# Output projection and feed-forward with activations stationary and 512 weight columns moving, norms by token row

## The chip, the cores and the metric

The kernel runs on one core of one Trainium2 chip. The metric is device time in microseconds for one execution; the time before is the median of three runs. Durations inside the execution come from the hardware profiler's record of one execution. The engines are named as the profile names them: PE (matrix products), PEld (its weight loads), DVE (vector), ACT (activation), POOL, and SP, whose queue issues the DMAs here.

## The reference

One layer of a decoder trunk over 256 tokens and 2048 channels, float32, with weights that are read once from HBM. What is computed, shortened:

```
mod = silu(c) @ w_mod + b_mod                       # 6 x 2048 values, from one vector c
sh1, sc1, g1, sh2, sc2, g2 = split(mod, 6)
u = x * (1 + sc1) + sh1
y = token_mixer(u)                                  # u @ w_in, mLSTM and HGRN2 heads, then ... @ w_out (2048 x 2048)
x = layer_norm(ALPHA * x + (1 + g1) * y, ln1_g, ln1_b)
u = x * (1 + sc2) + sh2
y = (silu(u @ w_gate) * (u @ w_up)) @ w_down        # 2048 x 5632 twice, 5632 x 2048
out = layer_norm(ALPHA * x + (1 + g2) * y, ln2_g, ln2_b)
```

Each product in float32 is made of three: an operand is split into a high part (rounded to fp32r) and a low part (the rest), and high x high, high x low and low x high are summed in PSUM.

## The kernel before

**Stages.** The input projection and the two head groups come first (the tile names `uh`, `ul`, `wh`, `wl`, `q`, `kk`, `pr`); then the output projection from `yh`, `yl` (high and low part of the mixer's output), the first norm, the modulation that makes `u2`, the feed-forward in two halves of 22 blocks of 128 hidden channels (gate and up first, then down), the second norm and the output.

**Weights.** Every weight tile is 128 x 1024 (512 KB). `wtile` (L206) lets SP fetch it into `wr`, ACT makes the high part `wh` from it (recorded at L128, the helper `act`), and DVE the low part `wl` by a subtraction (L213). There are 4 buffers for `wr`, 4 for `wh` and 3 for `wl`.

**Matrix products.** In the output projection and the feed-forward the weights are stationary, 128 x 128 at a time, and 256 tokens of activations move: `gB` (L243, matmuls L249 to L251), and the same three matmuls written out at L859 to L861 (the first 8 blocks of the feed-forward) and L872 to L874 (the others). Values are therefore held by channel: a channel is a partition, a token a column. `gA` (L253, matmuls L260 to L262) is the other form: 128 tokens of activations are stationary, 512 weight columns move; before the change only the parts `i` and `v` of the input projection use it.

**Norms.** As channels lie on partitions, a norm over channels needs sums across partitions: class `Norm` makes them by matmuls with a matrix of ones in plain float32 (L733, L774, L776) and applies them with L817 and L819 (first norm) or L903 and L904 (second).

**The modulation products.** The 96 values per partition of `mod` come one column at a time: `mod(j)` (L171) fetches 128 x 2048 of `w_mod` (1 MB) into one of 2 buffers `m`, and one DVE instruction (L174) multiplies it with `silu(c)` and sums. Columns 0 to 31 belong to u, 32 to 47 and 64 to 79 to the first gate and the second scale (`modq`, drawn by `mods_some` at rates RATE per step), 48 to 63 to the second shift (`make_u2`), 80 to 95 to the second gate, which only the feed-forward's down part needs.

**Order.** No order is written out by hand. A scheduler sorts the instructions of each engine by priorities, dependencies and its own estimate of times when the program is built; each engine then runs its list in that order, and SP issues its DMAs in one list as well. So where the 96 modulation products stand on DVE and in SP's list is the scheduler's result.

Of the kernel before, what the change touches and what calls it, by code (L numbers as in the profile page):

```python
# [9 lines left out]
P = 128  # L10
# [44 lines left out]
RATE = (0.3, 0.2, 0.3)  # L55
CFG = dict(big=10, med=10, wr=4, mr=2, wh=4, wl=3, s5=2, t=3, cm=2)
# [23 lines left out]
def build(nc, tc, d):  # L80
    from contextlib import ExitStack

    with ExitStack() as ctx:
# [70 lines left out]
        for n in (128, 256, 768, 2048):  # L154
            ones[n] = cst.tile([P, P], F32, name=f"ones{n}")
            nc.gpsimd.memset(ones[n], 1.0 / n)
# [527 lines left out]
        wo = [0]  # L684

        def next_wo():
            i = wo[0]
            wo[0] += 1
            return (wraw if i // 4 % 2 == 0 and i % 4 in NATIVE[i // 8] else wtile)(d["wo"][i])

        xa = [A(name="xa") for _ in range(2)]
        for i in range(4):
            o = xa[i // 2][:, 1024 * (i % 2) : 1024 * (i % 2) + 1024]
            nc.sync.dma_start(o, d["x"][i])
            act(o, o, AF.Copy, scale=ALPHA)
        z = [A(name="z") for _ in range(2)]

        def b8(ap, n=8):
            return ap.rearrange("p (o t) -> p o t", o=1).broadcast_to([P, n, T])

        class Norm:
            def __init__(self, z, base, gcol, dve):
                self.z, self.base, self.gcol, self.dve = z, base, gcol, dve
                self.todo = []
                self.n = 0

            def put(self, b, bank):
                for j in range(2):
                    o = kt(self.z, b + j)
                    stt(o, bank[:, j * T : j * T + T], self.gcol(b + j), kt(self.base, b + j), ALU.mult, ALU.add)  # L710
                if b == 4:
                    self.todo.append(self.shift)
                if b == 6:
                    self.shifted()
                    for k in range(0, 8, 2):
                        self.todo.append(lambda k=k: self.sums(k))
                if b >= 8:
                    self.todo.append(lambda: self.sums(b))

            def tick(self):  # L720
                for f in self.todo:
                    f()
                self.todo = []

            def total(self, o, n, tiles, first=True, last=True):
                if self.dve and len(tiles) > 2:
                    a = S(T, "t", bufs=CFG["t"])
                    tt(a, tiles[0], tiles[1], ALU.add)
                    for t in tiles[2:]:
                        tt(a, a, t, ALU.add)  # L730
                    tiles = [a]
                for i, t in enumerate(tiles):
                    mm(o, ones[n], t, start=first and i == 0, stop=last and i == len(tiles) - 1, skip_group_check=True)  # L733

            def shift(self):
                s = ps()
                self.total(s[:, :T], 768, [kt(self.z, k) for k in range(6)])
                self.sh = M(T, name="nsh")
                act(self.sh, s[:, :T], AF.Copy)

            def shifted(self):
                for t in (self.z[0], self.base[1]):
                    for i in range(0, 2048, 512):
                        v = v3(t[:, i : i + 512], 2)
                        tt(v, v, b8(self.sh, 2), ALU.subtract)

            def sums(self, b):
                if b == 0:
                    self.mu, self.ss = ps(), ps()
                    self.ma = self.sa = None  # L750
                    if self.dve:
                        t = M(512, name="nacc")
                        self.ma, self.sa = t[:, :T], t[:, T:]
                q = S(512, "s5", bufs=CFG["s5"])
                act(q, self.z[b // 8][:, (b % 8) * T : (b % 8) * T + 512], AF.Square)
                zs = [kt(self.z, b), kt(self.z, b + 1)]
                qs = [q[:, :T], q[:, T:]]
                if self.dve and b < 14:
                    if b == 6:
                        tt(self.ma, zs[0], zs[1], ALU.add)  # L760
                    elif b > 6:
                        for x in zs:
                            tt(self.ma, self.ma, x, ALU.add)
                    if b == 0:
                        tt(self.sa, qs[0], qs[1], ALU.add)
                    else:
                        for x in qs:
                            tt(self.sa, self.sa, x, ALU.add)
                    return
# [42 lines left out]
        def make_u2(k):  # L812
# [7 lines left out]
            if k == 0:  # L820
                table["first"] = i
# [150 lines left out]
```

## Time and profile before

| | |
|---|---|
| three runs | 1304.82, 1308.33, 1306.6 us; median 1306.6 |
| profiled execution: span from first to last instruction | 1303.7 us (no other time of this execution is listed) |
| PE / DVE / ACT busy | 1258.4 / 911.6 / 615.6 us |
| mean TensorE clock granted | 0.991 of 2.4 GHz |
| HBM read | 320.59 MB, 248 GB/s over the span |

The page divides the span into 40 slices and gives the busy share of each engine in tenths. A record of a matmul lasts longer than the distance to the next one, because matmuls are pipelined; how fast PE works is read from the starts of neighbouring records, not from the duration of one. A plain float32 matmul leaves two records. In a chain of records of one kind the timeline merges neighbours and writes xN.

### The profile page before, as it was taken

The numbers are of one execution on the slowest core, as the hardware profiler recorded it, in microseconds if no ns is written. First come the engines' busy times: TensorE is split into PE (matmuls) and PEld (weight loads), VectorE is DVE, ScalarE is ACT, GpSimd is POOL, SyncE is SP. The second block draws the span as 40 slices with busy tenths as digits, with TensorE's granted clock in tenths as the row PEclk, the third lists the DMA queues.
The fourth block names the chain that finished last, engine by engine and source line by source line (L and its number), as shares of the span: only waits on it lengthen the run. The fifth ranks groups of instructions, "written<-read, shape, count | busy, mean of one in ns | idle before, by whom it ended". The sixth has DMA issues, their size and how long they took to land.

```text
span 1303.7 us, 24455 instructions
## 1 busy us (share of the span) xinstructions
PE 1258.4 (97%) x10184; PEld 1224.8 (94%) x10184; DVE 911.6 (70%) x1079; ACT 615.6 (47%) x810; POOL 4.1 (0%) x15
## 2 busy tenths in 40 slices
PE   4899999999999999999999999999999999999995
PEld 4889999898989999999999999999999999999995
DVE  6779977999898897998876544444544544545755
ACT  4564446546655633654444443333444444443444
POOL 0000000000000000000000000000000000000000
PEclk9899999999999999999999999999999999999998
DMA  9988997756988889699896556656555656556561
GB/s 368 373 339 335 350 387 260 253 184 203 347 292 324 330 323 327 239 322 339 307 345 223 184 173 184 186 179 190 189 179 181 190 179 182 189 171 183 178 190 73
DMA packets 76863, 324.28 MB, mean 249 GB/s; under 512 B 8528, under 2 KB 8912, under 8 KB 64336
## 3 DMA queue, kind: packets, MB, share of 16 engines
q1 hardware_dynamic: 76752, 322.73, 71.6%
q8 instruction: 79, 1.29, 0.4%
q14 instruction: 32, 0.26, 0.1%
HBM read 320.59 MB, written 2.10 MB: 248 GB/s over the span
## 4 chain that ended last, share of the span: by engine, by line
PE 93%; DVE 4%; ACT 1%; issue 1%; DMA 1%; ACTq 0%; DVEq 0%
PE ps L249 14%; PE ps L251 14%; PE ps L250 14%; PE ps L874 11%; PE ps L873 11%; PE ps L872 11%; PE ps L860 2%; PE ps L861 2%; PE ps L859 2%; PE ps L261 2%; PE ps L260 2%; PE ps L262 2%; DVE m L174 2%; PE ps L445 1%; DVE wl L213 1%
## 5 line engine op out<-in xcount | busy, mean ns | idle before, releaser
L213 DVE TENSOR_TENSOR wl<-wr,wh 128x1024 fp32r<-128x1024 f32 (+1 forms) x416 | 498.5, 1203 | 326.9 <-PE ps L874 154.3
L128 ACT ACTIVATE wh<-wr 128x1024 fp32r<-128x1024 f32 (+1 forms) x416 | 432.6, 1042 | 541.1 <-PE ps L250 223.5
L872 PE MATMUL ps<-wh,wh 128*128 128x256 f32 x1152 | 326.0, 283 | 0.0
L873 PE MATMUL ps<-wl,wh 128*128 128x256 f32 x1152 | 326.0, 283 | 0.0
L874 PE MATMUL ps<-wh,wl 128*128 128x256 f32 x1152 | 326.0, 283 | 0.0
L174 DVE CUSTOM_DVE_ANT_0 m<-m,cb,init 128x2048 f32<-128x2048 f32 x96 | 225.0, 2347 | 15.1 <-DMA m<-in_wmod 14.7
L872 PEld LDWEIGHTS ps<-wh,wh 128*128 128x128 f32 x1152 | 221.2, 192 | 0.0
L873 PEld LDWEIGHTS ps<-wl,wh 128*128 128x128 f32 x1152 | 221.2, 192 | 0.0
L874 PEld LDWEIGHTS ps<-wh,wl 128*128 128x128 f32 x1152 | 221.2, 192 | 0.0
L249 PE MATMUL ps<-uh,wh 128*128 128x256 f32 x640 | 185.1, 294 | 22.0 <-ACT wh L128 16.8
L249 PE MATMUL ps<-h,wh 128*128 128x256 f32 x704 | 199.4, 283 | 0.0
L251 PE MATMUL ps<-h,wl 128*128 128x256 f32 x704 | 199.2, 283 | 0.0
L250 PE MATMUL ps<-h,wh 128*128 128x256 f32 x704 | 199.2, 283 | 0.0
L250 PE MATMUL ps<-ul,wh 128*128 128x256 f32 x640 | 182.3, 287 | 0.0
L251 PE MATMUL ps<-uh,wl 128*128 128x256 f32 x640 | 181.0, 288 | 1.1 <-DVE wl L213 1.0
L249 PEld LDWEIGHTS ps<-uh,wh 128*128 128x128 f32 x640 | 124.3, 196 | 24.7 <-ACT wh L128 17.2
L250 PEld LDWEIGHTS ps<-h,wh 128*128 128x128 f32 x704 | 135.2, 192 | 0.0
L249 PEld LDWEIGHTS ps<-h,wh 128*128 128x128 f32 x704 | 135.2, 192 | 0.0
L251 PEld LDWEIGHTS ps<-h,wl 128*128 128x128 f32 x704 | 135.2, 192 | 0.0
L250 PEld LDWEIGHTS ps<-ul,wh 128*128 128x128 f32 x640 | 125.2, 196 | 1.1 <-issue 1.0
L251 PEld LDWEIGHTS ps<-uh,wl 128*128 128x128 f32 x640 | 123.8, 195 | 2.0 <-DVE wl L213 1.8
L859 PE MATMUL ps<-wh,wh 128*128 128x256 f32 x256 | 71.6, 284 | 2.9 <-ACT wh L128 2.9
(203 smaller groups left out, 1484.5 us busy)
## 6 DMA issues: line engine op xcount, KB each, us to landing
m<-in_wmod SPq DMA_DIRECT2D x96, 1024.0 KB, 6.9
wr<-in_wg SPq DMA_DIRECT2D x144, 512.0 KB, 3.6
wr<-in_win SPq DMA_DIRECT2D x112, 512.0 KB, 5.3
wr<-in_wd SPq DMA_DIRECT2D x80, 512.0 KB, 3.5
wr<-in_wo SPq DMA_DIRECT2D x32, 512.0 KB, 5.0
wr<-in_wf SPq DMA_DIRECT2D x32, 512.0 KB, 5.2
wr<-in_wd SPq DMA_DIRECT2D x16, 256.0 KB, 2.6
xT<-in_x SPq DMA_DIRECT2D x4, 512.0 KB, 7.8
```

The source lines that it names most:

```text
L128: i = nc.scalar.activation(out, in_, f, **kw).ins
L174: table["mod"] = nc.vector.tensor_tensor_reduce(t, t, cb, 1.0, init[:, j : j + 1], ALU.mult, ALU.add, modc[:, j : j + 1]).ins
L213: tt(l[:, :m], r[:, :m], h[:, :m].bitcast(F32), ALU.subtract)
L249: mm(o, h[:, wsl], kt(uh, k0 + k), start=st, stop=False, skip_group_check=True)
L250: mm(o, h[:, wsl], kt(ul, k0 + k), start=False, stop=False, skip_group_check=True)
L251: mm(o, l[:, wsl], kt(uh, k0 + k), start=False, stop=en, skip_group_check=True)
L260: mm(o, a, h[:, w], start=first and k == 0, stop=False, skip_group_check=True)
L261: mm(o, a, l[:, w], start=False, stop=False, skip_group_check=True)
L859: mm(o, h[:, wsl], kt(u2h, k), start=k == 0 and w == 0, stop=False, skip_group_check=True)
L872: mm(o, h[:, wsl], kt(u2h, kk), start=kk == 0 and w == 0, stop=False, skip_group_check=True)
L873: mm(o, h[:, wsl], kt(u2l, kk), start=False, stop=False, skip_group_check=True)
L874: mm(o, l[:, wsl], kt(u2h, kk), start=False, stop=kk == KT - 1, skip_group_check=True)
```

## The change

- In the output projection and the feed-forward the operands change places. `three` (L709) takes 128 tokens of activations as the stationary operand and moves 512 columns of the weights, with two matmuls for the high part of the weights (L712, L713) and one for the low part (L716). Each of the two token halves t has banks of its own.
- Values are now held by token: a token is a partition. The residual is made by rows (`resid`, L723 with L725 or L727), the sums of the norm by DVE's statistics instructions (L730, L734), and the norm is applied by rows (L792, L935, L936). `z` holds x by rows. The ones-matrix matmuls of both norms go.
- A gate that was a column is now needed along the row: `bcast` (L689, L694) lays it out over 128 partitions by 16 plain float32 matmuls.
- The next product needs channels on partitions again, so PE transposes: 8 x 4 tiles for u2 (`make_u2`, L799) and 4 x 2 tiles for each of the 11 groups of 512 hidden channels (`flip`, L835).
- Skew: the last column group of the output projection does token half 0 before half 1; the first two k-steps of the feed-forward run for half 0 before half 1's u2 is made; the last two k-steps of the down part too.
- The feed-forward goes group by group: groups 0 and 1 together in 8 banks, then one group at a time; the down part follows groups 0 to 5 and then 6 to 10. The layer norm's weights come along the row by a broadcasting DMA (`spill`).
- RATE goes from (0.3, 0.2, 0.3) to (0.4, 0.3, 0.4); `wh` and `wl` get 5 buffers each, `s5` 4.

```diff
-RATE = (0.3, 0.2, 0.3)
-CFG = dict(big=10, med=10, wr=4, mr=2, wh=4, wl=3, s5=2, t=3, cm=2)
+RATE = (0.4, 0.3, 0.4)
+CFG = dict(big=10, med=10, wr=4, mr=2, wh=5, wl=5, s5=4, t=3, cm=2)
...
-        n1 = Norm(z, xa, lambda k: col(2, k), False)
-        for half in range(2):
-            banks = [ps() for _ in range(4)]
...
+        def three(banks, h, l, a, b, first, last):
+            for i, o in enumerate(banks):
+                w = slice(512 * i, 512 * i + 512)
+                mm(o, a, h[:, w], start=first, stop=False, skip_group_check=True)
+                mm(o, b, h[:, w], start=False, stop=False, skip_group_check=True)
+            for i, o in enumerate(banks):
+                w = slice(512 * i, 512 * i + 512)
+                mm(o, a, l[:, w], start=False, stop=last, skip_group_check=True)
...
+        def norm(t):
+            mv = S(4, f"mv{t}", bufs=1)
+            nc.vector.bn_aggr(mv[:, 0:2], st[t])
+            act(mv[:, 2:3], mv[:, 1:2], AF.Ln, bias=eps)
+            table["var"] = act(mv[:, 3:4], mv[:, 2:3], AF.Exp, scale=-0.5)
+            return mv[:, 0:1], mv[:, 3:4]
...
         run(modq)
...
+        for k in range(EARLY):
             run(mod(48 + k))
-            if k >= EARLY:
-                tc.add_manual_dep(table["mod"], table["first"].name, order, reason="norm")
...
+        def make_u2(t, c):
+            bank = ps()
+            for j in range(4):
+                nc.tensor.transpose(bank[:, P * j : P * j + P], z[t][:, 512 * c + P * j : 512 * c + P * j + P], ident)
+            for j in range(4):
+                k = 4 * c + j
+                if t == 0 and k >= EARLY:
+                    run(mod(48 + k))
+                    tc.add_manual_dep(table["mod"], table["first"].name, order, reason="norm")
+                o = bank[:, P * j : P * j + P]
+                h = u2(u2h, k, t)
+                act(h, o, AF.Identity, scale=Ac[:, k : k + 1], bias=col(3, k))
+                u = S(P, "t", bufs=CFG["t"])
+                ts(u, o, Ac[:, k : k + 1], col(3, k), ALU.mult, ALU.add)
+                tt(u2(u2l, k, t), u, h.bitcast(F32), ALU.subtract)
...
+        norm1(0)
+        use = False
+        for c in range(4):
+            make_u2(0, c)
+        norm1(1)
...
+        bk, held, block = ffn_in((0, 1))
+        for k in range(2):
+            for g in range(2):
+                held[k, g] = w1(d["wf"][g * KT + k])
+            block(k, 0)
+        for c in range(4):
+            make_u2(1, c)
+        for k in range(2):
+            block(k, 1)
+        for k in range(2, KT):
+            for g in range(2):
+                held[k, g] = w1(d["wf"][g * KT + k])
+            for t in range(2):
+                block(k, t)
...
+        up_to(range(2, 6))
+        G2 = bcast(5)
+        down(0, 24, G2, False)
+        up_to(range(6, NG))
+        use_set(AF.Exp)
+        Lg, Lb = spill("l2g"), spill("l2b")
+        down(24, 44, G2, True)
```

How the scheduler lays this out is told by the order of the two programs. First DVE in the kernel before, at the seam between the output projection and the feed-forward: `wl` is the low part of a weight tile (the first row is the feed-forward's third), L710 the last residual, L782 to L819 the norm, L826 the low part of u2, L174 a modulation product.

```order
L213 TENSOR_TENSOR wl_5449<-wr_5446,wh_5448 128x1024
L710 SCALAR_TENSOR_TENSOR z_4228<-ps_4756,modc,xa_4218 128x256 x2
L782 TENSOR_TENSOR nrs_5335<-ps_4821,nrs_5335 128x256
L817 TENSOR_TENSOR z_4227<-z_4227,nmu_5334 128x256 x4
L819 TENSOR_TENSOR z_4227<-z_4227,nrs_5335 128x256 x4
...
L213 TENSOR_TENSOR wl_5479<-wr_5476,wh_5478 128x1024
L819 TENSOR_TENSOR z_4227<-z_4227,nrs_5335 128x256
L174 ISA m_5920,modc<-m_5920,cb,init 128x2048
L174 ISA modc 128x1
L213 TENSOR_TENSOR wl_5518<-wr_5515,wh_5517 128x1024
```

The third, fourth and fifth feed-forward tiles' low parts stand here with one modulation product among them. Now DVE in the changed kernel at the same seam: `wl_5248` is the low part of the feed-forward's fifth weight tile, `wl_5254` of its sixth; L723 with ps_4498 makes the last residual of token half 1, L792 applies the norm, L809 and L810 make u2's low part (`u2l_4928` holds four k of it), L884 scales z for the second residual.

```order
L706 TENSOR_TENSOR wl_5248<-wr_5245,wh_5247 128x1024
L727 SCALAR_TENSOR_TENSOR z_4228<-z_4228,s_4907 128x512
L723 TENSOR_TENSOR s_4911<-ps_4498,bc_4234 128x512
...
L792 TENSOR_SCALAR z_4228<-z_4228,mv_4956 128x512 x4
L174 ISA m_5011,modc<-m_5011,cb,init 128x2048
L174 ISA modc 128x1
L809 TENSOR_SCALAR t_4970<-ps_4964,sc,modc 128x128
L174 ISA m_5018,modc<-m_5018,cb,init 128x2048
...
L810 TENSOR_TENSOR u2l_4928<-t_5143,u2h_4924 128x128
L174 ISA m_5871,modc<-m_5871,cb,init 128x2048
...
L706 TENSOR_TENSOR wl_5254<-wr_5251,wh_5253 128x1024
```

Between the fifth tile's subtraction and the sixth's stand 100 rows, and no weight tile is among them: 14 modulation products, 50 instructions of 128 columns (L809, L810), 21 of 512 columns (a row with x4 counted four times) and four of the statistics. One more modulation product stands right after the last residual of half 0 (`s_4907`), ahead of the low parts of tiles 2 to 5.

Last PE in the changed kernel at this place: L716 with ps_4498 ends the output projection (half 1), L799 are the transposes of z_4228 (half 0) and z_4229 (half 1), u2h_4924 and u2l_4928 belong to k 0 to 3; wl_5092 is the low part of the feed-forward's first tile, wl_5248 of its fifth, wh_5253 the high part of its sixth, ps_5086 a bank of half 1.

```order
L716 MATMUL ps_4498<-wl_4856,yh_4210 128x512
L799 MATMUL ps_4964<-kc,z_4228 128x128 x4
...
L713 MATMUL ps_5081<-wh_5091,u2l_4928 128x512
...
L716 MATMUL ps_5082<-wl_5248,u2h_4924 128x512
L799 MATMUL ps_5158<-kc,z_4229 128x128 x4
...
L716 MATMUL ps_5086<-wl_5092,u2h_4924 128x512
...
L712 MATMUL ps_5083<-wh_5253,u2h_4924 128x512
```

From the end of the output projection to the first matmul with the sixth tile stand the 32 transposes and 45 feed-forward matmuls: tiles 1 to 5 with half 0 (30) and 15 with half 1. Before, all 8 banks followed the norm with the first k at once, and no transpose was between.

## Rows read from the trace of the kernel before

**Rows 1.** The page: busy time of each engine, and the span in 40 slices (tenths of busy time; PEclk is the granted clock).

```profile
PE 1258.4 (97%) x10184; PEld 1224.8 (94%) x10184; DVE 911.6 (70%) x1079; ACT 615.6 (47%) x810; POOL 4.1 (0%) x15
...
PE   4899999999999999999999999999999999999995
...
DVE  6779977999898897998876544444544544545755
...
PEclk9899999999999999999999999999999999999998
DMA  9988997756988889699896556656555656556561
```

**Rows 2.** Busy time of each engine in four stretches: start and end, length, then PE, PEld, DVE, ACT, POOL with counts, the granted clock, the share of the DMA engines, GB/s. They are about the output projection, the feed-forward, what follows it, and the time right after the feed-forward's start.

```profile
417.00:524.00 107.00, 104.36 (x812) 101.31 (x810) 89.73 (x110) 52.46 (x60) 0.00 (x0) 1.00 0.88 324
524.29:1286.70 762.41, 762.41 (x6339) 762.32 (x6340) 451.54 (x525) 329.18 (x397) 0.00 (x0) 1.00 0.64 208
1286.70:1303.70 17.00, 2.92 (x14) 1.91 (x12) 11.02 (x19) 10.35 (x21) 0.00 (x0) 0.71 0.32 124
...
525.34:529.56 4.22, 4.22 (x25) 4.22 (x24) 3.14 (x8) 3.33 (x5) 0.00 (x0) 0.60 0.00 0
```

**Rows 3.** PE in order of time (start, duration, engine, line, tiles, sizes): the first and the last of 44 single records in the feed-forward, 256 columns each.

```profile
999.84 0.28 PE L873 MATMUL ps<-wl,wh 128*128 128x256 f32 x1
...
1005.00 0.28 PE L874 MATMUL ps<-wh,wl 128*128 128x256 f32 x1
```

**Rows 4.** The same view in the input projection: the first and the last of 23 single records of the form with 512 weight columns moving.

```profile
328.83 0.39 PE L261 MATMUL ps<-wl,uh 128*128 128x512 f32 x1
...
333.82 0.39 PE L262 MATMUL ps<-wh,ul 128*128 128x512 f32 x1
```

**Rows 5.** The same view: plain float32 matmuls, which leave two records each, with the next instruction behind them; 128 columns (L492) and 256 columns (L733, the ones matrix).

```profile
309.79 1.05 PE L492 MATMUL ps<-q,kk 128*128 128x128 f32 x8
310.60 0.48 PE L260 MATMUL ps<-wh,uh 128*128 128x512 f32 x1
...
460.65 2.75 PE L733 MATMUL ps<-z,ones 128*128 128x256 f32 x12
463.05 0.47 PE L249 MATMUL ps<-yh,wh 128*128 128x256 f32 x1
```

**Rows 6.** The same view at the start of the output projection: the last mLSTM head's matmuls, the first output projection matmul, and the head's last sums.

```profile
413.64 0.36 PE L249 MATMUL ps<-yh,wh 128*128 128x256 f32 x1
...
416.47 0.61 PE L587 MATMUL ps<-s,ones 128*128 128x256 f32 x2
```

**Rows 7.** The same view at the seam: the last output projection matmul, the last norm sums, the first feed-forward matmuls with the idle time before them.

```profile
517.10 0.28 PE L251 MATMUL ps<-yh,wl 128*128 128x256 f32 x1
...
520.27 1.13 PE L776 MATMUL ps<-s,ones 128*128 128x256 f32 x4
524.29 1.22 PE L859 MATMUL ps<-wh,wh 128*128 128x256 f32 x8 [2.89 <-ACT wh L128]
```

**Rows 8.** DVE in order of time behind the seam: steps of 256 columns, then a modulation product with its read-out and the weight subtraction behind it.

```profile
521.85 1.42 DVE L817 TENSOR_TENSOR z<-z,nmu 128x256 f32<-128x256 f32 x4
523.19 1.42 DVE L819 TENSOR_TENSOR z<-z,nrs 128x256 f32<-128x256 f32 x4
...
530.19 2.35 DVE L174 CUSTOM_DVE_ANT_0 m<-m,cb,init 128x2048 f32<-128x2048 f32 x1
532.46 0.08 DVE L174 DVE_READ_ACCUMULATOR2_ANT modc<- 128x1 f32 x1
532.46 1.22 DVE L213 TENSOR_TENSOR wl<-wr,wh 128x1024 fp32r<-128x1024 f32 x1
533.60 1.09 DVE L826 TENSOR_TENSOR wl<-t,wh 128x256 fp32r<-128x256 f32 x3
```

**Rows 9.** DVE's modulation products early in the kernel, in order of time: the first and the last of eight that stand close together.

```profile
9.32 2.35 DVE L174 CUSTOM_DVE_ANT_0 m<-m,cb,init 128x2048 f32<-128x2048 f32 x1
...
37.51 2.35 DVE L174 CUSTOM_DVE_ANT_0 m<-m,cb,init 128x2048 f32<-128x2048 f32 x1 [0.17 <-DMA m<-in_wmod]
```

**Rows 10.** The page's DMA issues: size of one, median us from issue to landing.

```profile
m<-in_wmod SPq DMA_DIRECT2D x96, 1024.0 KB, 6.9
```

**Rows 11.** The end of the kernel in order of time, PE, DVE and ACT: the last feed-forward matmul, steps of 512 columns of the last norm, the last DVE and ACT records.

```profile
1286.58 0.28 PE L251 MATMUL ps<-h,wl 128*128 128x256 f32 x1
...
1295.67 1.28 DVE L903 TENSOR_TENSOR z<-z,nmu 128x512 f32<-128x512 f32 x2
1296.88 1.28 DVE L904 TENSOR_TENSOR z<-z,nrs 128x512 f32<-128x512 f32 x2
...
1298.80 0.69 DVE L904 TENSOR_TENSOR z<-z,nrs 128x512 f32<-128x512 f32 x1
...
1297.59 3.06 ACT L128 ACTIVATE z<-z,pk 128x256 f32<-128x256 f32 x6 [0.33 <-DVE z L904]
```

**Rows 12.** Groups of instructions by line, small ones: count, total busy us and mean ns, on DVE and ACT.

```profile
L807 DVE TENSOR_TENSOR sc<-pk,modc 128x16 f32<-128x16 f32 x1 | 0.2, 170 | 0.0
L897 DVE SCALAR_TENSOR_TENSOR z<-ps,modc,z 128x256 f32<-128x256 f32 x16 | 7.0, 476 | 0.0
L120 ACT ACT_TABLE_LOAD x11 | 14.1, 1283 | 0.9 <-PEq L964 0.7
```

More of the change, by code (lines that the diff above doesn't have):

```diff
@@ L701, in build @@
[L701 to L769, printed above, removed]
-                one = [self.ma] if self.dve else []
-                two = [self.sa] if self.dve else []
-                if b >= 6:
-                    for i, x in enumerate(one + zs):
-                        mm(self.mu[:, :T], ones[2048], x, start=(b == 6 or self.dve) and i == 0, stop=b == 14 and x is zs[1], skip_group_check=True)
-                for i, x in enumerate(two + qs):
-                    mm(self.ss[:, :T], ones[2048], x, start=(b == 0 or self.dve) and i == 0, stop=b == 14 and x is qs[1], skip_group_check=True)
-            def done(self):
-                mu, rs = M(T, name="nmu"), M(T, name="nrs")
-                act(rs, self.mu[:, :T], AF.Square)
-                act(mu, self.mu[:, :T], AF.Copy)
-                table["var"] = tt(rs, self.ss[:, :T], rs, ALU.subtract).ins
-                act(rs, rs, AF.Ln, bias=eps)
-                act(rs, rs, AF.Exp, scale=-0.5)
-                return mu, rs
@@ new lines, in build, with resid, stat @@
+        st = [S(24, f"st{t}", bufs=1) for t in range(2)]
+        def resid(t, c, bank, gate, scale):
+            w = slice(512 * c, 512 * c + 512)
+            m = S(512, "s5", bufs=CFG["s5"])
+            tt(m, bank, gate[:, w], ALU.mult)
+            if scale is None:
+                tt(z[t][:, w], z[t][:, w], m, ALU.add)
+            else:
+                stt(z[t][:, w], z[t][:, w], scale, m, ALU.mult, ALU.add)
+        def stat(t, c):
+            nc.vector.bn_stats(st[t][:, 6 * c : 6 * c + 6], z[t][:, 512 * c : 512 * c + 512])
@@ new lines, in build, with u2, norm1 @@
+        u2l = [M(name="u2l", dt=F32R) for _ in range(4)]
+        def u2(tiles, k, t):
+            return tiles[k // 4][:, (k % 4) * T + t * P : (k % 4) * T + t * P + P]
+        for k in range(EARLY):
+            run(mod(48 + k))
+        def norm1(t):
+            mu, rs = norm(t)
+            for c in range(4):
+                w = slice(512 * c, 512 * c + 512)
+                i = ts(z[t][:, w], z[t][:, w], mu, rs, ALU.subtract, ALU.mult).ins
+                if t == 0 and c == 0:
+                    table["first"] = i
@@ new lines, in build, with spill, swi, flip @@
+        NG = DFF // 512
+        hid = {}
+        rows = {}
+        def spill(name):
+            o = A(name="bc")
+            nc.sync.dma_start(o, d[name].broadcast_to([P, D]))
+            return o
+        def swi(g, t, gate, up):
+            s = S(512, "s5", bufs=CFG["s5"])
+            act(s, gate, AF.Silu)
+            tt(s, s, up, ALU.mult)
+            rows[g, t] = s
+        def flip(g):
+            hd = A(F32R, name="hid")
+            hid[g] = hd
+            for b in range(2):
+                bank = ps()
+                for t in range(2):
+                    for j in range(2):
+                        nc.tensor.transpose(bank[:, j * T + t * P : j * T + t * P + P], rows[g, t][:, (2 * b + j) * P : (2 * b + j) * P + P], ident)
+                w = slice(512 * b, 512 * b + 512)
+                split(hd[:, w], hd[:, 1024 + 512 * b : 1536 + 512 * b], bank)
@@ new lines, in finish @@
+        def finish(t):
+            mu, rs = norm(t)
+            for c in range(4):
+                w = slice(512 * c, 512 * c + 512)
+                stt(z[t][:, w], z[t][:, w], mu, Lg[:, w], ALU.subtract, ALU.mult)
+                stt(z[t][:, w], z[t][:, w], rs, Lb[:, w], ALU.mult, ALU.add)
+                nc.sync.dma_start(d["out"][t][:, w], z[t][:, w])
+        up_to(range(2, 6))
[3 more added lines that the diff above has]
+        use_set(AF.Exp)
```

256 lines of the change are left out of this document (129 added, 127 removed).

## The prediction

> **What bounds the kernel now.** I read the page first. The reader is to see there that PE is busy 97% of the span, at nine tenths in all slices but the first two and the last, with the granted clock at full level in nearly all, while DVE runs mostly at 7 to 9 tenths in the first half and at 4 to 5 in the second [rows 1]. So PE bounds the second half alone; in the first half DVE and the DMA engines (9 tenths there too) follow close behind it, and a change there may hand the lead to them. Then the view by stretches: the feed-forward takes 762.4 us with PE busy all the time (6339 records, 0.120 us each) and DVE 451.5; behind it lie 17.0 us in which PE has 2.9 us of work; around the output projection the DMA engines are 88% busy at 324 GB/s [rows 2].
>
> Busy PE is not PE at its peak, so third I read starts in order of time. With 256 columns moving, 44 matmuls start in 43 steps of (1005.00 - 999.84) / 43 = 0.1200 us [rows 3]. The form with 512 columns, which the kernel already uses in the input projection, steps by (333.82 - 328.83) / 22 = 0.2268 us [rows 4]. Two narrow ones cost 0.2400. From the two rows: 0.417 ns per column, and 13.2 ns that each matmul costs whatever its width. The change saves that fixed part on every second matmul.
>
> **The stream.** The feed-forward has 6336 narrow matmuls (4224 for gate and up, 2112 for down); they become 3168 wide ones, 3168 x 0.2268 = 718.5 us. Against 762.4 that is -43.9. Nothing hides it and nothing else is late in the steady part: a weight tile lasts 12 x 0.2268 = 2.72 us on PE and needs 1.14 us of DVE [rows 8].
>
> Here a page speaks against the change. The rows show 13.2 ns of fixed cost at both widths [rows 3, 4]. The Trainium skill ("TensorE: Matmul & The Clock Gate", section "Wait — 56ns, not 53.3ns?") states that a warm matmul takes its columns at 2.4 GHz and about 2.5 ns more. By that rule the 3552 pairs of both stages would give back 3552 x 2.5 ns = 9 us, as an estimate, where the rows give 47. The trace does not agree, in either form, and the rows decide; what would have to be true for the small gain is the third rival.
>
> **New PE work.** 120 transposes (32 for u2, 88 for the hidden rows) and 16 float32 matmuls for the second gate's row. The trace has no full transpose. The nearest row is a plain float32 matmul with 128 columns: 0.81 us for eight records, 0.101 each [rows 5]. A transpose as one such record gives 12.1 us; the gate, two records per matmul, 3.2. Sum +15.3. Ends for the transposes: 0.067 each if they run like the stream (128 x 0.417 + 13.2 ns), 0.202 if they leave two records: 8 to 24 us. I take the middle, as the one row with float32 operands of this size.
>
> **Output projection.** Before, it goes from 413.64 to 521.40 (520.27 + 1.13): 107.8 us, with the ones-matrix sums of the norm in it, a dozen records of which take 2.4 us [rows 5 to 7]. Now PE's list has half the first gate's row, the last head's sums, the other half, then 384 wide matmuls. The head's sums cannot be earlier than now, 2.83 us after 413.64 [rows 6]; with 0.9 for them, 1.6 for half of 3.2, and 384 x 0.2268 = 87.1, the end is 92.4 us after 413.64: -15.4. But 35.7 MB have to come in that stage (32 weight tiles, 16 modulation tiles, x by rows; 34.6 before, both counted in SP's lists), and at the 324 GB/s of [rows 2] that takes 110 us, not 92. Much of it is asked for before the stage begins, since DVE's lists have 55 modulation products done by the last tile of the input projection in both programs. I take -13, ends -15.4 and 0.
>
> **The seam, where the price is.** DVE works through its list in order. Its place to start from is the residual of half 0's last bank, 24 wide matmuls (5.4 us) before the output projection ends. From there to the low part of the feed-forward's sixth weight tile stand, by the order of the changed kernel: 15 modulation products at 2.27 us (530.19 to 532.46), 5 weight subtractions at 1.14 (532.46 to 533.60) [rows 8]; 22 instructions of 512 columns and 2 statistics of 512, which the trace lacks and which I count like the others, at 0.605 (1.21 for two) [rows 11]; 50 of 128 columns at 0.20, the line through 0.605 for 512 and 0.335 for 256 (1.34 for four) [rows 8, 11]; two small ones at 0.17 [rows 12]. That is 34.1 + 5.7 + 14.5 + 10.0 + 0.3 = 64.6 us, and 1.4 for PE's last result to reach DVE and for logarithm and exponential on ACT; the table load of 1.28 [rows 12] lies beside a modulation product. So tile 6 is ready 66 us after the start. PE has for that time the 24 matmuls, 45 of the feed-forward (10.2) and the 32 transposes (3.2): 18.8 us. It is idle for 47.
>
> Why nothing else can go ahead: all of half 1's first matmuls wait in PE's list for transposes that need a bank which DVE frees late, the sixth tile waits for a weight buffer which half 1's matmuls free, and SP's list has 13 modulation tiles between the feed-forward's ninth and tenth weight tile (none before the change). Behind tile 6 DVE needs 22.8 us for the next eight tiles with four more modulation products, and PE has 27.9 us of work saved up: I add 2 for waits between. The clock: after 2.9 us of idle time now it is 0.60 for 4.2 us [rows 2], 1.7 us lost; I take 2. For the modulation tiles' transfers I add 3: DVE asks for one every 3.3 to 3.6 us, and eight early ones came 4.03 us apart ((37.51 - 9.32) / 7) with weight tiles on the same engines [rows 9]. Together 54, against the 2.9 us of now [rows 7]: +51.1. Ends: 41 (128 columns at half the price, no waits, no lost clock) and 67 (two buffers at the 6.9 us of [rows 10] and 2.35 of work: 4.6 per product).
>
> **The end.** After the last matmul DVE has 28 steps of 512 columns for both halves (16.9 us), of which it may start 2.7 us (12 matmuls) early; with 1.3 for waits and statistics and 1 for scalars taken from a column (a 256-column instruction of that kind lasts 476 ns, [rows 12], the plain ones 0.42) it ends 16.5 us after PE. Before, the last ACT record ends at 1300.65, 13.9 after PE's last stream matmul, and 3.05 before the span ends [rows 2, 11]. So +2.6; the skew's gain is used up since DVE does what ACT shared. Ends 0 and +5.
>
> **Sum.** -43.9 + 15.3 - 13 + 51.1 + 2.6 = +12.1. The profiled span is 1303.7, so 1315.8; the median of the runs lies 2.9 above that span (1306.6), and with the same around it the forecast is 1319 us. The rest I cost at nothing: the input projection keeps its instructions, and a few more buffers and modulation products moved by two weight tiles lie under PE's 98%; should that cover go, some 3 us either way.
>
> **Rivals.**
> First, the other side: PE's own chain sets the seam and the list's fill does not. Then half 0 starts when its first u2 is there, 21.8 us after the start (the same prices up to that row), so 16 us of idle time instead of 47, and the modulation products would have to fall into gaps. Seam 18 - 2.9 = 15.5, time 1283. For it: the first five tiles need nothing that stands later. Against: the sixth does, and an engine that runs its list in order cannot pull it forward. It decides from where idle and lost time at the seam stay under 42 us, the sum being zero there.
> Second, the modulation tiles' transfers pace the seam: 4.6 us each for 15, 69 us, with some 10 of other work ahead of the first: 79 instead of 66, less the 3 I put in: 1329. For it the 0.17 us waits for m in [rows 9]; against it SP then fetches hardly anything else.
> Third, the wide form does not save its fixed part in these stages, as consecutive matmuls here change stationary tile and bank in another pattern than in [rows 4]. Of 47 us 9 would be left: 1357. Against it stand the equal 13.2 ns of two patterns.
> Fourth, the prices at the seam near their low end and transposes at 0.067: -10 - 4, about no change, 1305.
>
> **Chances.** Forecast 0.66 (its own range 1308 to 1331), transfers 0.16, PE's own chain 0.09, fixed part 0.04, low prices 0.05. What a measurement of this kernel can tell from no change is 0.3%, about 4 us: 1302.7 to 1310.5. Slower: forecast 0.57, transfers 0.16, fixed part 0.04, 0.77. Same: 0.07 of the forecast, 0.04 of the low prices, 0.11. Faster 0.12: PE's chain 0.09, and 0.03 from the low ends. The range leaves out the fixed part and most of the first rival: 1302 to 1340.
>
> **What would show it.** Right: starts of L712 0.227 us apart in the feed-forward; between PE's last output projection matmul and a steady stream some 50 us of idle time put down to DVE (u2l, then wl), with L174 filling DVE and the clock at half level in part of it; DVE's stretch there at ten tenths; nearly 20 us after the last matmul. Wrong: a seam under 42 us, transposes that start 0.2 us apart, steps of 0.24, or weight tiles late in the output projection.

## The result, and the profile after

| | before | after |
|---|---|---|
| median of the runs, us | 1307.3 (4 runs, 1304.8 to 1308.3) | 1317.5 (4 runs, 1315.6 to 1319.0) |
| span of the profiled execution, us | 1303.7 | 1313.8 |
| mean granted clock of TensorE | 0.991 | 0.972 |

The change makes the kernel slower: ratio 1.0081, 95% interval 1.0065 to 1.0096. The span grows by 10.1 us.

The page of the changed kernel first, as in [rows 1]: busy time, then the slices of PE, DVE and the clock, then the chain that ended last.

```profile
PE 1222.5 (93%) x6738; PEld 1048.4 (80%) x6738; DVE 913.0 (69%) x1026; ACT 585.3 (45%) x728; POOL 3.9 (0%) x13
...
PE   4899999899999996289999999999999999999994
DVE  6789997999998799997845444445455444445555
...
PEclk9999999899999998689999999999999999999997
...
PE 86%; DVE 8%; DMA 2%; issue 2%; ACT 1%; DVEq 0%; SPq 0%; ACTq 0%
```

PE has 36 us less work than in [rows 1] (1222.5 against 1258.4) and the kernel is still later. Three slices of PE in the middle, which were nines before, read 6, 2, 8; DVE has nines there, and the clock falls with PE. That is the seam. The view by stretches gives the sizes: output projection, seam, the steady feed-forward, and what lies behind it.

```profile
413.00:506.00 93.00, 93.00 (x429) 77.53 (x428) 81.04 (x93) 44.20 (x50) 0.00 (x0) 1.00 0.89 329
506.00:586.00 80.00, 37.72 (x136) 28.84 (x136) 78.27 (x132) 22.26 (x43) 0.00 (x0) 0.70 0.79 289
586.00:1294.00 708.00, 708.00 (x3184) 587.61 (x3184) 376.11 (x352) 295.24 (x303) 0.00 (x0) 1.00 0.63 200
1294.00:1313.80 19.80, 0.76 (x4) 0.29 (x2) 16.19 (x27) 1.00 (x4) 0.00 (x0) 0.60 0.29 106
```

In the 80 us of the seam PE is busy for 38, DVE for 78, at a mean clock of 0.70. In the stretches before and behind it PE never stops until its last matmul. PE's waits in that stretch, by what released them (total, times, longest):

```profile
PE ps L799 <- DVE t L809: 18.1, 2, 13.7
PE ps L712 <- DVE t L809: 9.8, 2, 6.1
PE ps L799 <- DVE z L792: 9.6, 1, 9.6
PE ps L716 <- DVE wl L706: 2.4, 1, 2.4
PE ps L713 <- DVE u2l L810: 2.0, 1, 2.0
PE ps L712 <- ACT wh L128: 0.3, 1, 0.3
```

That is 42.2 us of idle time in all. The same stretch in order of time, from the last output projection matmul on, where [rows 7] showed 2.89 us of waiting:

```profile
505.79 0.39 PE L716 MATMUL ps<-wl,yh 128*128 128x512 f32 x1
515.77 3.68 PE L799 MATMUL ps<-kc,z 128*128 128x128 f32 x16 [9.59 <-DVE z L792]
519.10 1.43 PE L712 MATMUL ps<-wh,u2h 128*128 128x512 f32 x4
522.54 0.81 PE L713 MATMUL ps<-wh,u2l 128*128 128x512 f32 x2 [2.01 <-DVE u2l L810]
...
530.67 0.60 PE L799 MATMUL ps<-kc,z 128*128 128x128 f32 x4
535.64 1.12 PE L799 MATMUL ps<-kc,z 128*128 128x128 f32 x4 [4.37 <-DVE t L809]
550.45 1.11 PE L799 MATMUL ps<-kc,z 128*128 128x128 f32 x4 [13.69 <-DVE t L809]
557.70 0.79 PE L712 MATMUL ps<-wh,u2h 128*128 128x512 f32 x1 [6.13 <-DVE t L809]
...
565.07 0.79 PE L712 MATMUL ps<-wh,u2h 128*128 128x512 f32 x1 [3.69 <-DVE t L809]
565.66 0.63 PE L713 MATMUL ps<-wh,u2l 128*128 128x512 f32 x1
...
569.50 0.63 PE L712 MATMUL ps<-wh,u2h 128*128 128x512 f32 x1
...
585.74 0.96 PE L716 MATMUL ps<-wl,u2h 128*128 128x512 f32 x3 [2.45 <-DVE wl L706]
```

Three things are to be seen. The waits of 4.37 and 13.69 us, the second the longest of all, are those of half 1's transposes for a bank: half 0's last banks come free when DVE has made t from them. The later ones of 6.13 and 3.69 us are those of half 1's first products for the banks that half 1's own transposes filled, which come free with half 1's fourth and eighth t. And after a wait the wide matmuls start 0.43 us apart for a while instead of 0.227 (nine steps from 565.66 to 569.50). Summed over the seam, each record's distance to the next less its distance at full clock gives 53.4 us lost: 42.2 idle and 11.2 slow.

What DVE does meanwhile, in order of time: the residual that opens the seam, and the stretch in which PE waits 13.69 us.

```profile
501.61 0.67 DVE L723 TENSOR_TENSOR s<-ps,bc 128x512 f32<-128x512 f32 x1
...
536.32 2.34 DVE L174 CUSTOM_DVE_ANT_0 m<-m,cb,init 128x2048 f32<-128x2048 f32 x1
...
538.59 0.68 DVE L885 SCALAR_TENSOR_TENSOR z<-bc,z 128x512 f32<-128x512 f32 x1
539.19 0.41 DVE L809 TENSOR_SCALAR t<-ps,sc,modc 128x128 f32<-128x128 f32 x1
539.51 2.34 DVE L174 CUSTOM_DVE_ANT_0 m<-m,cb,init 128x2048 f32<-128x2048 f32 x1
...
549.99 0.72 DVE L809 TENSOR_SCALAR t<-ps,sc,modc 128x128 f32<-128x128 f32 x2
...
567.94 2.35 DVE L706 TENSOR_TENSOR wl<-wr,wh 128x1024 fp32r<-128x1024 f32 x2
```

One modulation product after another, with the small instructions of u2 and the affine steps on z (L884, L885) between them; DVE waits for a transfer for 1.2 us in the whole seam:

```profile
DVE m L174 <- DMA m<-in_wmod: 1.2, 2, 0.9
```

The low part of the sixth weight tile, the first of the last row's two, is ready at 569.1, 67.5 us after 501.61.

### The profile page after: what moved, and what is told of

Same layout as the page of the kernel before. It is cut to its first block, busy times and chain, and to the rows that moved or that the text cites. A ratio compares the mean times of both kernels' runs of the same rounds, so it can differ in the third digit from the quotient of the medians.

```text
span 1313.8 us, 17232 instructions
## 1 busy us (share of the span) xinstructions
PE 1222.5 (93%) x6738; PEld 1048.4 (80%) x6738; DVE 913.0 (69%) x1026; ACT 585.3 (45%) x728; POOL 3.9 (0%) x13
## 4 chain that ended last, share of the span: by engine, by line
PE 86%; DVE 8%; DMA 2%; issue 2%; ACT 1%; DVEq 0%; SPq 0%; ACTq 0%
PE ps L716 20%; PE ps L713 20%; PE ps L712 20%; PE ps L249 5%; PE ps L251 5%; PE ps L250 5%; DVE m L174 4%; DMA m<-in_wmod 2%; PE ps L260 2%; PE ps L261 2%; PE ps L262 2%; PE ps L445 1%; DVE wl L213 1%; PE ps L835 1%; DVE wl L706 1%
## 5 line engine op out<-in xcount | busy, mean ns | idle before, releaser
L128 ACT ACTIVATE wh<-wr 128x1024 fp32r<-128x1024 f32 x408 | 431.1, 1059 | 569.7 <-PE ps L713 426.9
L706 DVE TENSOR_TENSOR wl<-wr,wh 128x1024 fp32r<-128x1024 f32 x296 | 361.5, 1225 | 327.5 <-ACT wh L128 326.9
L712 PE MATMUL ps<-wh,u2h 128*128 128x512 f32 x704 | 277.2, 394 | 10.1 <-DVE t L809 9.8
L713 PE MATMUL ps<-wh,u2l 128*128 128x512 f32 x704 | 276.0, 393 | 2.0 <-DVE u2l L810 2.0
L174 DVE CUSTOM_DVE_ANT_0 m<-m,cb,init 128x2048 f32<-128x2048 f32 x96 | 225.1, 2346 | 10.5 <-DMA m<-in_wmod 10.1
L716 PE MATMUL ps<-wl,u2h 128*128 128x512 f32 x704 | 220.4, 393 | 2.5 <-DVE wl L706 2.4
L712 PEld LDWEIGHTS ps<-wh,u2h 128*128 128x128 f32 x704 | 133.6, 190 | 39.0 <-DVE t L809 10.7
L716 PEld LDWEIGHTS ps<-wl,u2h 128*128 128x128 f32 x704 | 133.3, 190 | 31.3 <-DVE wl L706 3.3
L713 PEld LDWEIGHTS ps<-wh,u2l 128*128 128x128 f32 x704 | 133.6, 190 | 30.1 <-DVE u2l L810 2.4
L213 DVE TENSOR_TENSOR wl<-wr,wh 128x1024 fp32r<-128x1024 f32 x112 | 135.8, 1221 | 27.0 <-ACT wh L128 26.4
L712 PE MATMUL ps<-wh,hid 128*128 128x512 f32 x352 | 137.2, 390 | 0.0
L713 PE MATMUL ps<-wh,hid 128*128 128x512 f32 x352 | 137.0, 389 | 0.0
L716 PE MATMUL ps<-wl,hid 128*128 128x512 f32 x352 | 108.4, 389 | 0.0
L713 PEld LDWEIGHTS ps<-wh,hid 128*128 128x128 f32 x352 | 66.1, 188 | 13.7
L716 PEld LDWEIGHTS ps<-wl,hid 128*128 128x128 f32 x352 | 66.1, 188 | 13.7
L712 PEld LDWEIGHTS ps<-wh,hid 128*128 128x128 f32 x352 | 66.1, 188 | 13.6
```

The lines of the kernel that those rows point to most:

```text
L128: i = nc.scalar.activation(out, in_, f, **kw).ins
L174: table["mod"] = nc.vector.tensor_tensor_reduce(t, t, cb, 1.0, init[:, j : j + 1], ALU.mult, ALU.add, modc[:, j : j + 1]).ins
L213: tt(l[:, :m], r[:, :m], h[:, :m].bitcast(F32), ALU.subtract)
L706: tt(l, r, h.bitcast(F32), ALU.subtract)
L712: mm(o, a, h[:, w], start=first, stop=False, skip_group_check=True)
L713: mm(o, b, h[:, w], start=False, stop=False, skip_group_check=True)
```

## The experiments

All are edits of the changed kernel (1317.5 us, ratio 1.0081). Theory: DVE's time for what stands in its list at the seam sets the loss. Rivals: PE's own chain; the modulation tiles' transfers. "Lost" is the sum over the seam made as above, idle and slow together. The scheduler lays every build out anew: the output projection's first wide matmul starts between 418.85 us (changed kernel) and 422.15. The times contain that, the lost time does not.

**Hold the second gate's products back.**

```diff
-            tt(s, s, up, ALU.mult)
+            table["swi", g, t] = tt(s, s, up, ALU.mult).ins
...
                         run(mod(mods.pop(0)))
+                        tc.add_manual_dep(table["mod"], table["swi", 0, 0].name, order, reason="swi")
```

> Modulation products 80 to 95 (second gate) may only run on DVE after the activation product of the feed-forward's groups 0 and 1. Theory (DVE's list sets the seam): five of them leave the list ahead of the sixth weight tile's low part and the first tiles behind it; by the prices of the trace the list up to that row gets 8 us shorter, and the 2.5 us wait for a low part behind it goes too: 1306 to 1310 us, 8 to 12 below the changed kernel, with less idle time put down to t and wl at the seam. Rival 1 (PE's own chain sets the seam): no change, 1315 to 1320. Rival 2 (modulation tiles' transfers set it): 15 to 20 below, since five transfers of 1 MB leave the seam at up to 4.6 us each.

Measured 1305.4 us, ratio 0.9985 (0.9971 to 0.9999): 12.1 below the changed kernel, just past the theory's 8 to 12 and short of the second rival's 15 to 20. 41.3 us are lost, 33.3 of them idle. (The profiled spans differ by 9.8 only, since in this build the output projection's first wide matmul starts 2.1 us later.) Its waits at the seam:

```profile
PE ps L799 <- DVE t L809: 18.6, 2, 14.2
PE ps L799 <- DVE z L792: 9.9, 1, 9.9
PE ps L712 <- DVE t L809: 2.8, 1, 2.8
PE ps L713 <- DVE u2l L810: 2.0, 1, 2.0
```

The later waits for t fall from 9.8 to 2.8 and the one for wl goes; the waits of half 1's transposes stay, since products 56 to 63 are still ahead of them. PE's own chain as what sets the seam falls here. The transfers could still do this.

**Transfers without DVE's time, DVE's time without transfers.** Two kernels take the two apart.

```diff
-            nc.sync.dma_start(t, d["wmod"][j])
-            table["mod"] = nc.vector.tensor_tensor_reduce(t, t, cb, 1.0, init[:, j : j + 1], ALU.mult, ALU.add, modc[:, j : j + 1]).ins
+            late = 56 <= j < 64 or j >= 80
+            if not late:
+                nc.sync.dma_start(t, d["wmod"][j])
+            table["mod"] = nc.vector.tensor_tensor_reduce(t, cb if late else t, cb, 1.0, init[:, j : j + 1], ALU.mult, ALU.add, modc[:, j : j + 1]).ins
```

> Modulation products 56 to 63 and 80 to 95 keep their DVE instruction but read a tile that is already in SBUF: their 24 transfers of 1 MB are left out (their columns are then not the reference's). Theory (DVE's time for the products sets the seam): nearly no change, 1310 to 1318 us; the list up to the sixth low part is 4 us shorter in this build's order. Rival 2 (transfers set the seam): 20 to 30 us below the changed kernel, 1288 to 1298. Rival 1 (PE's own chain): no change.

```diff
+            n = 128 if 56 <= j < 64 or j >= 80 else D
-            table["mod"] = nc.vector.tensor_tensor_reduce(t, t, cb, 1.0, init[:, j : j + 1], ALU.mult, ALU.add, modc[:, j : j + 1]).ins
+            table["mod"] = nc.vector.tensor_tensor_reduce(t[:, :n], t[:, :n], cb[:, :n], 1.0, init[:, j : j + 1], ALU.mult, ALU.add, modc[:, j : j + 1]).ins
```

> The same 24 products keep their transfers of 1 MB, but the DVE instruction works on 128 of the 2048 columns (the columns are then not the reference's). Theory (DVE's time sets the seam): the list up to the sixth low part falls from 59 to about 36 us by the trace's prices, the later wait goes and some of the half-clock time: 22 to 32 us below the changed kernel, 1286 to 1296, idle time of PE at the seam from 42 to 15 to 22 us. Rival 2 (transfers): no change or some us, 1310 to 1318. Rival 1 (PE's own chain): no change.

Without the transfers: 1309.3 us, ratio 1.0019 (1.0007 to 1.0030), 45.6 lost. With the transfers and short instructions: 1294.0, ratio 0.9905 (0.9889 to 0.9921), 30.2 lost, 23.2 of them idle, where 15 to 22 idle were expected:

```profile
PE ps L800 <- DVE t L810: 11.5, 2, 9.5
PE ps L800 <- DVE z L793: 9.4, 1, 9.4
PE ps L713 <- DVE t L810: 2.3, 1, 2.3
```

The 24 transfers of 1 MB give back 8 us when they go, DVE's time 23.5 while they stay. DVE's time is the larger cause by far. The 8 us lie just outside the theory's range, which ended at 1310; 4 of them were priced from that build's shorter list, the rest is not separated between waits for tiles and the changed order.

**Both left out.**

> Modulation products 56 to 63 and 80 to 95 are left out, transfers and instructions both; their columns hold the bias alone. Theory (DVE's time for them sets the seam, transfers at most a few us): 2 to 6 us below the version that keeps the transfers and shortens the instruction (1294.0), whose short instructions still take DVE 0.3 us each: 1288 to 1292. Rival (transfers cost as much as the instructions once these are short): 1280 or less.

Measured 1287.8 us, ratio 0.9856 (0.9837 to 0.9874), 23.0 lost. It is 6.2 below the version with short instructions, just past the expected 2 to 6. So even without any of these 24 products the seam costs 23 us: 9.6 until the first normalised quarter is there, the rest half 1's waits and slow matmuls.

**Narrow matmuls again.**

```diff
             for i, o in enumerate(banks):
-                w = slice(512 * i, 512 * i + 512)
-                mm(o, a, h[:, w], start=first, stop=False, skip_group_check=True)
+                for v in (0, 256):
+                    w = slice(512 * i + v, 512 * i + v + 256)
+                    mm(o[:, v : v + 256], a, h[:, w], start=first, stop=False, skip_group_check=True)
...
```

> Every matmul with 512 moving weight columns in the output projection and the feed-forward is made as two with 256 columns, in the same order, operands and banks; all else stays. Theory (each matmul costs 13.2 ns beside its columns, whatever its width): 3552 more matmuls, 46.9 us more, 1358 to 1366 us, steps of 0.120 us in the feed-forward. Rival (the wide form does not pay): by a fixed part of 2.5 ns, as the Trainium skill (TensorE: Matmul & The Clock Gate) gives it, 9 us more, about 1326.

In this form the sums in the banks are not the reference's, and the runs do not show why; every wide matmul is two narrow ones, as told. Measured 1355.9 us, ratio 1.0379 (1.0363 to 1.0394): 38.3 above the changed kernel by the medians and 41.8 by the profiled spans (1355.6), where 46.9 was expected. The Trainium skill's rule ("TensorE: Matmul & The Clock Gate", section "Wait — 56ns, not 53.3ns?") would have made it 9, as an estimate. Pairs of matmuls start 0.24 us apart, so one takes 0.1200:

```profile
1000.06 0.40 PE L713 MATMUL ps<-wh,u2h 128*128 128x256 f32 x2
1000.30 0.40 PE L716 MATMUL ps<-wh,u2l 128*128 128x256 f32 x2
```

The step is as expected, so the fixed 13.2 ns are confirmed. The miss is in the sum: at the seam 46.8 us are lost instead of 53.4 (37.4 of them idle instead of 42.2), and the output projection's first matmul starts 1.9 us later. Together that is 4.7 of the 5.1 us by which the spans fall short. So "all else stays" did not hold: in this build no modulation product stands on DVE between half 0's last residual and the first normalised quarter, where the changed kernel has two, and PE's wait before the first transposes is 5.5 us instead of 9.6.

**Hold the affine steps back as well** (on top of the first version).

```diff
-            stt(z[t][:, w], z[t][:, w], ALPHA, Ag[:, w], ALU.mult, ALU.mult)
+            i = stt(z[t][:, w], z[t][:, w], ALPHA, Ag[:, w], ALU.mult, ALU.mult).ins
+            tc.add_manual_dep(i, table["swi", 0, 0].name, order, reason="swi")
```

> As the version with products 80 to 95 held back (1305.4 us), and the preparation of the second residual (the two instructions per 512 columns that apply the first norm's weights to z for later use) also waits in DVE's list for the activation product of groups 0 and 1. Theory (whatever stands in DVE's list ahead of half 1's u2 and the sixth low part is paid at the seam): the list up to the sixth low part falls from 51 to 42 us, so 1295 to 1300 us, 6 to 10 below that version. Rival (half 1's own chain of transpose, u2 and bank sets the seam by now): 0 to 2 below it.

Measured 1302.8 us, ratio 0.9969 (0.9957 to 0.9982); 38.6 lost against 41.3. That is 2.6 below the version before: the theory's 6 to 10 failed, and the rival's 0 to 2 is the nearer. DVE's waits between 506 and 560 us, of which the version before has only the last:

```profile
DVE t L809 <- ACT u2h L128: 2.6, 8, 0.5
DVE m L174 <- DMA m<-in_wmod: 0.7, 2, 0.5
DVE z L792 <- ACT mv L128: 0.5, 1, 0.5
```

In the version before, eight affine steps (4.8 us at 0.60) stood ahead of half 0's last t. Once they are gone, DVE waits there for ACT and for transfers instead (1.8 of the 3.3 us in the first two rows lie ahead of that t), and that t starts 1.3 us sooner after the residual, 46.8 us against 48.1; the rest of the 4.8 is not separated. Three more stood between it and half 1's fourth t, and what stands there weighs less: PE's wait there falls from 2.8 to 2.3 us only. So the list does not set the seam by its length up to the sixth low part. What PE waits for is half 0's last t, and then half 1's first ones, and taking the affine steps out ahead of them gains little.

**Draw products 48 to 63 earlier** (on top of the first version).

```diff
-RATE = (0.4, 0.3, 0.4)
+RATE = (0.6, 0.45, 0.6)
...
-        modq = chain(*[mod_pe(PE_SECT.index(s), s) if s in PE_SECT else chain(*[mod(16 * s + k) for k in range(16)]) for s in (2, 4)])
+        modq = chain(*[mod_pe(PE_SECT.index(s), s) if s in PE_SECT else chain(*[mod(16 * s + k) for k in range(16)]) for s in (2, 4, 3)])
...
-        for k in range(EARLY):
-            run(mod(48 + k))
...
```

> As the version with products 80 to 95 held back, and products 48 to 63 are drawn during the input and output projections like 32 to 47 and 64 to 79, with RATE (0.6, 0.45, 0.6). By the built order six products leave the seam and the list up to the sixth low part falls from 51 to 43 us. Theory: the seam gets 6 to 9 us shorter, but the stages before it are asked for six more transfers of 1 MB and 14 us more of DVE, which they have only in part: 1296 to 1305 us in all, with the output projection's end 0 to 8 us later. Rival (those stages have no room at all): all is given back, 1303 to 1310.

Here the second shift lacks one term (the norm's bias times the second scale), because its products run before that term is there. Measured 1299.1 us, ratio 0.9938 (0.9923 to 0.9953): inside the theory's range. 29.7 us are lost at the seam, 11.6 less, but the output projection ends at 511.9 instead of 508.2: a third of the gain is paid upstream. With products 56 to 63 away, PE's waits for t fall from 21.4 to 7.7 us, while the one for the first normalised quarter grows from 9.9 to 16.9.

**Make u2 in quarters, between the weight tiles of one group** (on top of the version with both held back).

```diff
         norm1(0)
-        use = False
-        for c in range(4):
-            make_u2(0, c)
+        make_u2(0, 0)
         norm1(1)
+        make_u2(1, 0)
...
-        bk, held, block = ffn_in((0, 1))
...
+                    if g == 0 and k in (1, 5, 9):
+                        for t in range(2):
+                            make_u2(t, k // 4 + 1)
...
-        up_to(range(2, 6))
+        up_to(range(0, 6))
```

> As the version with both held back, and the feed-forward's first group runs alone in four banks, with each quarter of u2 made for both halves just ahead of the k-steps that need it (quarters 1, 2 and 3 after steps 1, 5 and 9), no skew at its start. Products 56 to 63 then stand between weight tiles and not ahead of the first ones. Theory: by the prices DVE's list is through group 0 after 59 us, of which PE has 47 us of work; 12 to 20 us are lost at the seam instead of 52: 1280 to 1292 us. Rival (many short waits, one per quarter and half, each with lost clock): 1295 to 1303.

Measured 1294.4 us, ratio 0.9901 (0.9884 to 0.9918). It is the best so far of the versions that leave nothing out, but lies above the theory's range, close to the rival's. 27.5 us are lost, 19.3 of them idle, in waits for u2l (9.7 us in four) and z (9.6 in two). DVE, which the price took as busy throughout, waits itself:

```profile
DVE wl L706 <- ACT wh L128: 4.0, 5, 1.1
DVE m L174 <- DMA m<-in_wmod: 1.9, 1, 1.9
```

**t on ACT**, in that version and alone in the changed kernel.

```diff
-                ts(u, o, Ac[:, k : k + 1], col(3, k), ALU.mult, ALU.add)
+                act(u, o, AF.Identity, scale=Ac[:, k : k + 1], bias=col(3, k))
```

> As the version by quarters, and the scaled and shifted value t that the low part of u2 is made from is made by ACT instead of DVE (32 instructions of 128 columns, 0.32 us each on DVE). Theory: DVE's list up to the end of group 0 falls from 59 to 49 us, PE's 47 us of work are then nearly the bound: 5 to 10 us below the version by quarters, 1273 to 1284. Rival (ACT makes wh and both parts of u2 and becomes the late one): no change against the version by quarters or some us slower.

> The changed kernel with one edit: t, from which the low part of u2 is made, comes from ACT instead of DVE (32 instructions of 128 columns). The place of everything else is the scheduler's. Theory (DVE's list up to half 0's last t and half 1's u2 sets the seam): the list up to the sixth low part falls from 59 to 47 us by the trace's prices: 8 to 14 us below the changed kernel, 1303 to 1309. Rival (what made this edit worth 18.7 us in the version by quarters is ACT's order or the clock and not DVE's time): 15 to 20 below, 1297 to 1302. Rival (ACT as late as DVE): no change.

By quarters: 1275.7 us, ratio 0.9766 (0.9749 to 0.9784), 12.3 lost, 9.6 of them idle until the first z. The time lies in the expected 1273 to 1284, but only because the version by quarters had itself come out slower than expected: the edit is worth 18.7 there, not 5 to 10. Alone: 1303.2 us, ratio 0.9974 (0.9964 to 0.9985), 38.8 lost. That is 14.3 below the changed kernel, between the theory's 8 to 14 and the first rival's 15 to 20. The waits of the edit alone tell where its gain lies, with one row of ACT ahead of the longest wait's end:

```profile
PE ps L799 <- ACT t L128: 21.1, 2, 13.8
PE ps L712 <- ACT t L128: 1.3, 1, 1.3
...
550.75 0.46 ACT L128 ACTIVATE u2h<-ps,modc,sc 128x128 fp32r<-128x128 f32 x1 [3.00 <-DVE modc L174]
```

The waits of half 1's transposes stay (21.1 us, 18.1 in the changed kernel), and the last of these transposes start 48.0 us after the residual, 48.8 there: half 0's last u2 needs the value of product 63 as its shift, and ACT, which is early, waits for that. The later waits go (for t from 9.8 to 1.3 us; those for u2l and wl are gone). So it is the products 56 to 63 themselves, which the kernel lets run only after the first norm step, that set when half 0's last bank comes free. The other versions bear this out: 48.6 us after the residual with the second gate's products held back, 39.0 with short instructions, 31.6 with products 56 to 63 and 80 to 95 left out.

One stretch of the version by quarters shows why the edit is worth more there:

```profile
520.00:570.00 50.00, 50.00 (x232) 41.41 (x232) 46.48 (x68) 38.22 (x75) 0.00 (x0) 1.00 0.85 303
```

Once its first quarter is there PE is never late again, so the 9.7 us of waits for u2l and the slow matmuls behind them go together (27.5 to 12.3); another 1.6 us come from an earlier start of the output projection, which makes the 16.8 by which the profiled spans differ. ACT, at 38 of 50 us, still has room. This version leaves nothing out and is faster than both kernels, by 2.3% against the one before.

## Why the prediction was right

The forecast was 1319, the time is 1317.5. Between the two profiled executions, by the prediction's terms:

| term | predicted, us | measured, us | from |
|---|---|---|---|
| stream | -43.9 | -43.9 | L712, L713 and L716 0.2267 apart in the steady stretch |
| new PE work | +15.3 | +16.0 | 120 transposes at 0.104, 32 records of the gate in 3.49 |
| output projection | -13 | -16.2 | 414.49 to 506.02 against 107.8 |
| seam: idle and slow | 54 - 2.9 | 53.4 - 2.9 | the sum above |
| end | +2.6 | +2.2 | last matmul, by its step, ends at 1294.60, span 1313.8: 19.2 against 17.0 |
| stages ahead | 0 | +0.85 | output projection starts at 414.49, before at 413.64 |
| not assigned | | +0.65 | the first matmul behind each set of transposes, rounding |
| sum | +12.1 | +10.1 | |

The rows for the stream and for the transposes are these: 150 steps in 34.00 us, and 16 transposes in 1.66 us.

```profile
959.94 0.39 PE L712 MATMUL ps<-wh,hid 128*128 128x512 f32 x1
...
993.94 0.39 PE L712 MATMUL ps<-wh,u2h 128*128 128x512 f32 x1
...
657.96 1.91 PE L835 MATMUL ps<-kc,s 128*128 128x128 f32 x16
659.62 0.49 PE L712 MATMUL ps<-wh,u2h 128*128 128x512 f32 x1
```

**The stream** holds, and the narrow form confirms its price from the other side: 0.1200 at 256 columns, 0.2267 at 512, in this kernel's own pattern. The Trainium skill ("TensorE: Matmul & The Clock Gate", section "Wait — 56ns, not 53.3ns?") gives a warm matmul about 2.5 ns beside its columns, and none when the clock is low. At half clock the trace agrees, 0.427 us for 512 columns at 1.2 GHz (nine steps from 565.66 to 569.50); at full clock it does not, 13.2 ns.

**The output projection** was mis-sized: -13 was taken and -16.2 came. The tiles for which 2.4 us had been allowed were not late: PE is busy for all of the stretch, with 384 matmuls in 87.2 us (418.85 to 506.02).

**The seam** came out in sum, not in its parts, so that the sum is met within 0.6 us is luck. Idle time was 47 + 2 and is 42.2; the low clock was 2 and is 11.2; the 3 us for transfers are not borne out (DVE waits 1.2 us for them). These errors cancelled. The prices of DVE's list were off both ways and cancelled in part too: L792 takes 0.46 per 512 columns, not 0.605; L809 takes 0.32 per 128, not 0.20. The sixth low part came 67.5 us after the start, 66 predicted. But it was named as the row that PE waits for, and that is wrong in mechanism: PE's last long waits end with half 0's last t and half 1's fourth and eighth, earlier in the same list, and the held-back affine steps show that other work between those rows is worth little. The sign that the idle time would be put down to u2l and then wl failed with it: these have 2.0 and 2.4 us, t has 27.9 and z 9.6. What was right is that DVE's list with its modulation products sets the seam, and that half 1's transposes wait for a bank which DVE frees late.

**The rivals.** PE's own chain as the seam's limit: out, holding back five products gives 12 us. Transfers: out as the main cause (8 us for all 24, against 23.5 for DVE's time). The wide form that does not pay: out by the narrow form. Low prices: idle and lost time lie at the middle of the range.

**The end.** The statistics take 0.60 per 512 columns as priced, L935 and L936 0.66:

```profile
1304.87 1.42 DVE L935 SCALAR_TENSOR_TENSOR z<-z,mv,bc 128x512 f32<-128x512 f32 x2
1306.20 1.41 DVE L936 SCALAR_TENSOR_TENSOR z<-z,mv,bc 128x512 f32<-128x512 f32 x2
```

## What to carry to other kernels

A change that speeds up the bounding engine in the steady stretch can lose all of it at one handover: look for the place where that engine must wait for results of another, and add up what the other engine's in-order list holds ahead of them. Work that is needed late should not stand there (12 us here), and work that is needed there should be asked for piece by piece, just ahead of its use, and spread over engines with room (27 us more here, from 1302.8 to 1275.7). When such a gap is priced, add the time in which the matmuls behind it run at half clock, and take as its end the row that frees what the waiting engine needs, a bank here, not a row farther down.

## What was not expected of the hardware

The gaps cost more than their own length. Behind the waits of 2 to 14 us at the seam the wide matmuls start 0.43 us apart, for instance from 565.66 to 570.78, before they return to 0.23. The granted clock there is 0.50, the 1.2 GHz level:

```profile
565.66:570.78 5.12, 5.12 (x13) 3.92 (x12) 5.12 (x7) 2.28 (x3) 0.00 (x0) 0.50 0.82 274
```

In all it is 11.2 us beside 42.2 us of idle time, where [rows 2] had one short stretch at 0.60. The version by quarters has 8.2 us of it beside 19.3, the one with t on ACT 2.7 beside 9.6.
